# The RWKV-7 state chain laid out over both halves of the TensorE array

## The chip, the core and the metric

The kernel runs on one core of a Trainium2 chip. Its engines are TensorE (PE in the profile, with its weight loads as PEld), VectorE (DVE), ScalarE (ACT), GpSimd (POOL) and the queue that issues DMAs (SP). Each works through its own list of instructions in order and waits on semaphores for the others. The metric is the time of one execution in device microseconds (us).

## What is computed

One layer over 4096 tokens of 1024 features: a conditioned RMS norm, one input projection, a pooling branch, an RWKV-7 branch of 8 heads of 64, an output projection, the residual and a last norm. The change lies in the RWKV-7 branch:

```python
def step(S, inp):                        # per head; S is 64 x 64
    r_t, w_t, k_t, v_t, am_t, b_t = inp  # am = -kk, b = kk * a
    sa = jnp.einsum('bhij,bhj->bhi', S, am_t)
    S = (S * w_t[:, :, None, :]
         + sa[..., None] * b_t[:, :, None, :]
         + v_t[..., None] * k_t[:, :, None, :])
    y = jnp.einsum('bhij,bhj->bhi', S, r_t)
    return S, y
```

## The kernel before

Phase 1 makes the normed input and the pooling branch. Phase 2, the RWKV-7 branch, goes through 16 blocks of 256 tokens, each of 4 chunks of 64. Phase 3, the output projection, is spread into the last block and the tail.

A block has four parts. `front(b)` projects the block's input into 17 tiles of 128 features (`pj`, lines 570 to 572: eight steps of three f16 matmuls each); a step is a unit of fill. It is a generator: units of `front(b + 1)` are issued inside the other parts of block b by `fill(n)`, and so stand between their matmuls. Behind each group of four tiles (k, r, v, z of a head pair) come small products (`pl`, `pa`, `vps`, `pb`). `scores(b)` (lines 685 to 716) makes the 64x64 score matrices. `inverse(b)` (lines 728 to 784) inverts 32 triangular matrices: 30 steps on DVE (lines 746 and 751), two DVE transposes, then the products `qp` (line 774) and `m21p` (line 782). `chain(b)` (line 786 on) carries the state through the four chunks.

In a chunk the chain takes the heads in two groups of four. For each group it clears half a PSUM bank with a matmul of zeros (line 798), adds V to the scores (line 801, weights from rows 64 to 127), and multiplies the stored state by A and R of a pair in one matmul of 128x128 (line 806); `S` holds two heads of a pair on its diagonal, with zero blocks beside them. ACT copies the result out (`xa`, line 811), PE multiplies by the inverse (line 820), ACT copies that into `UV` (line 825) and scales S (line 831). Then PE makes the addition to S (line 835), which DVE adds (line 839), and the output y (line 846), which ACT copies (line 850). Four of every eight heads' products of lines 801 and 846 go to the same 64 output columns.

PE's order is that of a scheduler which takes instructions by the order written and by what is ready in its own plan; it may split a group. The counts of fill units are FS, FT, FA, FM, FB, FY, FC and the list FI. `ps_x` has two PSUM banks (`px`), `ps_pj` three.

Of the kernel before, what the change touches and what calls it, by code (L numbers as in the profile page):

```python
# [20 lines left out]
P = 128  # L21
# [3 lines left out]
NH = 8  # L25
# [11 lines left out]
# columns of the packed per-feature vectors  # L37
# [15 lines left out]
def kernel(  # L53
# [83 lines left out]
    with ExitStack() as ph:  # L137
# [10 lines left out]
        # -- c @ w_ada + b_ada, features on partitions --  # L148
# [21 lines left out]
        # evacuation scales: 1/(s_h s_w); z's goes into u's, and silu's half too  # L170
# [18 lines left out]
        def row_scale(b, ss):  # L189
            """[P, 4] sums of the rows' squares -> rows' 1/rms, broadcast over partitions"""  # L190
# [63 lines left out]
        def prep_u(q):  # L254
            """pooling weights: w_u @ blockdiag(pool_w), split into fp16 halves"""
# [48 lines left out]
        def gain():  # L304
            # |x| * rstd <= sqrt(D) bounds |h|
# [63 lines left out]
        def prep_gate():  # L369
            """gate, broadcast over partitions"""  # L370
# [11 lines left out]
        def prep_wo(k):  # L382
            """gate folded into w_out's columns, in two float32r parts"""
# [39 lines left out]
        def pooled(b, g, pu, tz):  # L423
# [5 lines left out]
            # trailing sums by doubling  # L429
# [14 lines left out]
        def side(b):  # L444
            """the later phases' weights, prepared along the way"""
# [46 lines left out]
    # =====================================================================  # L492
    # phase 2: RWKV-7 branch
    # =====================================================================
    with ExitStack() as ph:
# [10 lines left out]
        # block-of-ones, centering and per-head selectors  # L506
# [12 lines left out]
        # score mask [(b/k, s), (a/r, t)]: s < t for a, s <= t for r  # L519
# [26 lines left out]
        zw = k2c.tile([P, 64], F32, name="zw")  # L546
        G.memset(zw, 0.0)
# [7 lines left out]
        def front(b, f):  # L555
# [9 lines left out]
            def seg(m, name, bufs=1):  # L565
                pp = ps_pj.tile([P, TB2 + 1], F32, tag="pj", name=f"pj{b}_{m}")
                for k in range(KT):
                    if k:
                        yield
                    PE.matmul(pp, w2_hi[m][:, k, :], hh[k], start=(k == 0), stop=False)  # L570
# [26 lines left out]
            for p in range(NPAIR):  # L597
# [8 lines left out]
                # decay  # L606
# [65 lines left out]
        def scores(b, f, fill):  # L672
            AR, BK = f["AR"], f["BK"]
            # 1 / max(|kk|^2, eps^2): tokens on partitions, and instances on partitions
# [4 lines left out]
            for ch in range(NCH):  # L679
                # the two heads of a pair in turn: they use different rows of the array  # L680
# [16 lines left out]
                fill(2 * FS)  # L697
# [24 lines left out]
        def inverse(b, f, fill):  # L722
            """MT[:, i, :] = transpose of (I - D A)^-1 D, A strictly lower 64x64, D diagonal,
            per instance. Its two 32x32 diagonal blocks by elimination, an instance and a half of the
            rows per lane; the block below the diagonal by two products."""
# [3 lines left out]
            # both diagonal blocks of A^T side by side, then instances onto partitions  # L729
# [39 lines left out]
            fill(FT)  # L769
            pt = ps_sc.tile([P, 512], F32, tag="sc", name=f"qp{b}")  # L770
# [14 lines left out]

        def chain(b, f, fill):
            AR, UV, sc, BT, pc = f["AR"], f["UV"], f["sc"], f["BT"], f["pc"]
            MT = UV[0:64].rearrange("q c (h t) -> q (c h) t", h=NH)
            for ch in range(NCH):
                pxs, xas = [], []  # L790
                psn = ps_s.tile([P, NPAIR, HS], F32, tag="psn", name=f"psn{b}_{ch}")
                if ch % 2 == 0:
                    y = blk.tile([P, 512], F32, tag="y", name=f"y{b}_{ch}", bufs=3)
                for g in range(2):
                    # columns 0:256: A^T S and its additions (rows a, r); 256:512: U
                    px = ps_x.tile([P, 512], F32, tag="px", name=f"px{b}_{ch}_{g}")
                    pxs.append(px)
                    PE.matmul(px[64:128, 511:512], zw, zw[:, 0:1], start=True, stop=True, skip_group_check=True)  # L798
                    for j in range(4):
                        h = 4 * g + j  # L800
                        PE.matmul(  # L801
# [240 lines left out]
```

## Time and profile before

| | |
|---|---|
| time, median of 3 runs | 2221.42 us (2218.44 to 2222.96) |
| the profiled execution, its span from the first instruction to the last | 2223.1 us |
| PE busy | 2129.8 us (96%) |
| DVE busy | 1432.6 us (64%) |
| ACT busy | 1225.1 us (55%) |
| phase 2, from the first scores to the last output of the chain | about 455 to 1913 us |

The profile gives no other time of the profiled execution than its span. An x8 in a row of the timeline counts matmul records: an f32 matmul leaves two of them (two passes over its columns), an f16 matmul one. A row's second number runs to the end of the last result, and results overlap with the next matmul's start, so what a group occupies on PE is read from its start to the start of the next row.

### The profile page before, as it was taken

Reading aid. Unit: us, or ns where it says so; the run is one execution under the profiler, and the core shown is the slowest. Engines: PE = TensorE matmul, PEld = TensorE weight load, DVE = VectorE, ACT = ScalarE, POOL = GpSimd, SP = SyncE. Lnnn points to the kernel's source line nnn. Section 1 sums busy time; section 2 is a strip of 40 time slices with the busy share of each in tenths; the row PEclk is TensorE's granted clock in tenths of the full one; section 3 lists DMA queues with packets and bytes.
Section 4 is the critical chain, followed back from the end, with each engine's and each line's share of the span. In section 5 each row is a group of like instructions: output and inputs, shape, how many; then the busy total and the mean of one; then the engine's idle time right before and its main releaser. Section 6 shows DMA issues by size and latency. Waiting matters only on the chain. (4 is left out here: it accounts for less than half of the span.)

```text
span 2223.1 us, 46475 instructions
## 1 busy us (share of the span) xinstructions
PE 2129.8 (96%) x18906; PEld 1620.5 (73%) x18906; DVE 1432.6 (64%) x3407; ACT 1225.1 (55%) x2924; POOL 153.2 (7%) x271
## 2 busy tenths in 40 slices
PE   4999999999999999999999999999999999999998
PEld 2444444787787877878778777787787877788887
DVE  8898967575756757658477575675765847443433
ACT  3545433466676676666766667667676664422211
POOL 3000000000000000000000000000000000000000
PEclk7999999999999999999999999999999989999999
DMA  7867677000010000100100001000010423444432
GB/s 277 282 227 252 223 238 241 15 20 25 7 30 21 11 26 6 30 25 6 30 11 20 25 6 30 17 15 26 6 30 25 138 77 120 148 139 145 138 109 75
DMA packets 140440, 183.08 MB, mean 82 GB/s; under 512 B 12097, under 2 KB 94017, under 8 KB 140226
## 3 DMA queue, kind: packets, MB, share of 16 engines
q1 hardware_dynamic: 140226, 180.11, 24.8%
q8 instruction: 148, 2.42, 0.5%
q14 instruction: 66, 0.54, 0.1%
HBM read 121.22 MB, written 58.85 MB: 81 GB/s over the span
## 5 line engine op out<-in xcount | busy, mean ns | idle before, releaser
L570 PE MATMUL pj<-hh,w2h 128*128 128x257 f16 x2176 | 601.8, 277 | 1.0 <-ACT up L427 0.8
L572 PE MATMUL pj<-hh,w2l 128*128 128x257 f16 x2176 | 595.1, 273 | 0.0
L571 PE MATMUL pj<-hl,w2h 128*128 128x257 f16 x2176 | 593.4, 273 | 0.0
L570 PEld LDWEIGHTS <-w2h 128*128 128x128 f16 x2176 | 211.5, 97 | 53.8
L571 PEld LDWEIGHTS <-w2h 128*128 128x128 f16 x2176 | 214.6, 99 | 26.7 <-issue 1.3
L572 PEld LDWEIGHTS <-w2l 128*128 128x128 f16 x2176 | 210.2, 97 | 31.9
L942 PE MATMUL po<-wo,mh 128*128 128x512 f32 x512 | 204.4, 399 | 1.7 <-ACT mh L926 1.7
L943 PE MATMUL po<-wo,mh 128*128 128x512 f32 x512 | 202.1, 395 | 0.0
L413 PE MATMUL pp<-lo,w1h 128*128 128x512 f16 x512 | 194.7, 380 | 0.8 <-DVE lo L225 0.8
L414 PE MATMUL pp<-hi,w1l 128*128 128x512 f16 x512 | 194.4, 380 | 0.0
L412 PE MATMUL pp<-hi,w1h 128*128 128x512 f16 x512 | 194.0, 381 | 0.3 <-ACT hi L224 0.3
L948 ACT ACTIVATE sq<-x 128x512 f32<-128x512 f32 x64 | 40.4, 631 | 202.5 <-DVE x L946 200.3
L946 DVE TENSOR_TENSOR x<-po,x 128x512 f32<-128x512 f32 x64 | 44.2, 691 | 155.4 <-PE po L944 155.2
L839 DVE TENSOR_TENSOR S<-psn,S 64x256 f32<-64x256 f32 x128 | 53.9, 421 | 128.1 <-PE psn L835 127.3
L746 DVE TENSOR_TENSOR Wt<-W,Ab 128x30 f32<-128x30 f32 (+7 forms) x480 | 118.7, 247 | 17.9 <-ACT W L741 8.5
L751 DVE TENSOR_TENSOR W<-W,Wt 128x30 f32<-128x30 f32 (+7 forms) x480 | 117.9, 246 | 8.2
L714 ACT ACTIVATE bc<-BK,pc 128x128 f32<-128x128 f32 x256 | 91.8, 397 | 48.1 <-PE btp L715 27.3
L942 PEld LDWEIGHTS po<-wo,mh 128*128 128x128 f32 x512 | 96.9, 189 | 23.6 <-ACT mh L926 2.0
L943 PEld LDWEIGHTS po<-wo,mh 128*128 128x128 f32 x512 | 96.7, 189 | 22.4
L831 ACT ACTIVATE S<-S,pc 128x128 f32<-128x128 f32 x256 | 95.2, 397 | 28.9 <-PE px L806 28.4
L944 PE MATMUL po<-wo,ml 128*128 128x512 f32 x256 | 101.7, 399 | 0.0
L414 PEld LDWEIGHTS <-w1l 128*128 128x128 f16 x512 | 50.3, 98 | 61.3 <-issue 2.1
(278 smaller groups left out, 4318.9 us busy)
## 6 DMA issues: line engine op xcount, KB each, us to landing
x<-in_x_dram SPq DMA_DIRECT2D x64, 256.0 KB, 3.0
out_dram<-x SPq DMA_DIRECT2D x64, 256.0 KB, 2.1
xk<-in_xT_dram SPq DMA_DIRECT2D x56, 256.0 KB, 3.8
xt<-in_x_dram SPq DMA_DIRECT2D x28, 512.0 KB, 5.6
wada<-in_w_ada_dram SPq DMA_DIRECT2D x24, 512.0 KB, 6.8
w2raw<-in_w_in_dram SPq DMA_DIRECT2D x17, 512.0 KB, 5.5
hh<-hT_hi SPq DMA_DIRECT2D x32, 257.0 KB, 3.4
hl<-hT_lo SPq DMA_DIRECT2D x32, 257.0 KB, 3.0
```

Source lines behind the costliest of these rows:

```text
L412: PE.matmul(pp, w1_hi[m][:, k, :], hi, start=(k == 0), stop=False)
L413: PE.matmul(pp, w1_hi[m][:, k, :], lo, start=False, stop=False)
L414: PE.matmul(pp, w1_lo[m][:, k, :], hi, start=False, stop=(k == KT - 1))
L570: PE.matmul(pp, w2_hi[m][:, k, :], hh[k], start=(k == 0), stop=False)
L571: PE.matmul(pp, w2_hi[m][:, k, :], hl[k], start=False, stop=False)
L572: PE.matmul(pp, w2_lo[m][:, k, :], hh[k], start=False, stop=(k == KT - 1))
L746: V.tensor_mul(tmp[:, :n, :k], W[:, r0:, k : k + 1].to_broadcast([P, n, k]), Ab[:, k : k + 1, :k].to_broadcast([P, n, k]),)
L751: V.tensor_add(W[:, r0:, :k], W[:, r0:, :k], tmp[:, :n, :k])
L831: A.activation(S[:, p, :], S[:, p, :], AF.Identity, bias=0.0, scale=pc[:, p, ch : ch + 1])
L942: PE.matmul(po, mh[:, k, ts_], wo[0][k][n], start=(k == 0), stop=False)
L943: PE.matmul(po, mh[:, k, ts_], wo[1][k][n], start=False, stop=False)
L944: PE.matmul(po, (ml[:, k] if b % 2 == 0 else ml[k])[:, ts_], wo[0][k][n], start=False, stop=(k == KT - 1))
```

## The change

The state S loses its zero blocks: for each head pair it is 128 partitions by 64 columns, the even head on the lower 64 partitions and the odd head on the upper 64. The two `px` banks now stand for even and for odd heads and stay for a whole block; chunks take turns in their two halves of 256 columns. Every product of the chain is one of 64 columns that uses a quarter of the array (or, for lines 860 and 867, half of it), and neighbours in the order use different quarters. A chunk has three visits to the array's small tiles: A and R by S (line 833); the inverse's product together with the V products of the next chunk (lines 846 and 808); the additions to S and y (lines 860 and 867). The V products of chunk 0 are issued in `inverse`, ahead of `qp`. The clearing matmuls are gone. U is written to the upper half of the `psn` bank. The chain's matmuls, and the first fill matmul behind each visit, are kept in program order. The counts of fill units are others.

```diff
-    FS, FT, FA, FM, FB, FY, FC = 2, 5, 2, 1, 0, 1, 0
-    FI = [5 + ((i + 1) * 0 // 10 - i * 0 // 10) for i in range(17)]
+
+    FS, FT, FA, FB, FY = 2, 5, 2, 2, 2
+    FI = [5 - i % 2 for i in range(17)]
...
-        S = k2c.tile([P, NPAIR, P], F32, name="S")
+        S = k2c.tile([P, NPAIR, HS], F32, name="S")
...
-                fill(2 * FS)
+                fill(FS + 1)
...
+            f["px"] = [ps_x.tile([P, 512], F32, tag="px", name=f"px{b}_{hf}") for hf in range(2)]
+            run(lead(b, f, 0))
...
+        def ordered(mm):
+
+            pin[0] = True
+            return tc.keep_in_program_order(mm)
...
+            UV, sc, (pe, po) = f["UV"], f["sc"], f["px"]
+            par = 256 * (ch % 2)
+            for p in range(NPAIR):
+                for hf, px in ((0, pe), (1, po)):
+                    h, o = 2 * p + hf, 64 * hf
+                    ordered(PE.matmul(
+                        px[o : o + 64, par + p * HS : par + (p + 1) * HS], sc[64:128, ch * NH + h, 0:64],
+                        UV[64:128, ch, h * HS : (h + 1) * HS], start=(p == 0), stop=False, skip_group_check=True,
+                    ))
+                yield
...
-                    PE.matmul(px[64:128, 511:512], zw, zw[:, 0:1], start=True, stop=True, skip_group_check=True)
...
-                    for q in range(2):
-                        PE.matmul(
-                            px[:, q * P : (q + 1) * P], AR[:, 2 * g + q, ch].rearrange("q a t -> q (a t)"),
-                            S[:, 2 * g + q, :], start=False, stop=(q == 1), skip_group_check=True,
-                        )
...
+                    for ar in range(2):
+                        for hf, px in ((0, pe), (1, po)):
+                            o, ro = 64 * hf, 64 * (hf ^ ar)
+                            ordered(PE.matmul(
+                                px[ro : ro + 64, cs], AR[o : o + 64, p, ch, ar, :], S[o : o + 64, p, :],
+                                start=(p == 0 and ar == 1), stop=(ar == 0), skip_group_check=True,
+                            ))
...
+                    A.copy(xa, px[64 * hf : 64 * hf + 64, par : par + 256])
...
+                nl = lead(b, f, ch + 1) if ch + 1 < NCH else iter(())
+                for p in range(NPAIR):
                     for hf in range(2):
...
+                        ordered(PE.matmul(
+                            psn[64 * hf : 64 * hf + 64, uo + p * HS : uo + (p + 1) * HS],
+                            MT[:, ch * NH + 2 * p + hf, :], xas[hf][:, p * HS : (p + 1) * HS],
+                            start=True, stop=True, skip_group_check=True,
+                        ))
+                    run(nl, 1)
...
-                for hf in range(2):
-                    o = 64 * hf
-                    sv = S[o : o + 64, :, o : o + 64]
-                    V.tensor_add(sv, psn[o : o + 64], sv)
...
+                V.tensor_add(S, psn[:, 0:uo].rearrange("q (j e) -> q j e", e=HS), S)
+                for h in range(NH):
+                    hf, o = h % 2, 64 * (1 - h % 2)
+                    ordered(PE.matmul(
+                        (pe, po)[hf][o : o + 64, par + (h // 2) * HS : par + (h // 2 + 1) * HS],
+                        sc[:, ch * NH + h, 64:128], UV[:, ch, h * HS : (h + 1) * HS],
+                        start=False, stop=True, skip_group_check=True,
+                    ))
...
-                fill(FC)
+                fill(FY)
```

Where the instructions stand. On PE, before, in chunk 1 of block 2, at the start of the chunk (`px2_1_0` and `px2_1_1` are the two groups' banks, `pj3_16` a tile of the next block's projection):

```order
L798 MATMUL px2_1_0_7865<-zw_3686 64x1
L801 MATMUL px2_1_0_7865<-UV2_5631,sc2_6856 64x64 x4
L806 MATMUL px2_1_0_7865<-S_3690,AR2_5627 128x128 x2
L798 MATMUL px2_1_1_7875<-zw_3686 64x1
L801 MATMUL px2_1_1_7875<-UV2_5631,sc2_6856 64x64 x4
L806 MATMUL px2_1_1_7875<-S_3690,AR2_5627 128x128 x2
L570 LDWEIGHTS w2h16_2196
```

On PE, now, in the same chunk, the end of the first visit (`px2_0` is the even heads' bank, `px2_1` the odd heads'):

```order
L833 MATMUL px2_0_7664<-S_3688,AR2_5647 64x64
L833 MATMUL px2_1_7665<-S_3688,AR2_5647 64x64
L568 LDWEIGHTS w2h14_2188
L568 MATMUL pj3_14_7794<-hh3_1_6916,w2h14_2188 128x257
L569 LDWEIGHTS w2h14_2188
```

The second visit in the same chunk:

```order
L570 MATMUL pj3_14_7794<-hh3_1_6916,w2l14_2189 128x257
L846 MATMUL psn2_1_7854<-xa2_1_0_7871,UV2_5651 64x64
L846 MATMUL psn2_1_7854<-xa2_1_1_7873,UV2_5651 64x64
L808 MATMUL px2_0_7664<-UV2_5651,sc2_6898 64x64
L808 MATMUL px2_1_7665<-UV2_5651,sc2_6898 64x64
L846 MATMUL psn2_1_7854<-xa2_1_0_7871,UV2_5651 64x64
```

Line 833 has 16 matmuls in a row there, line 846 eight with eight of line 808 between them; the fill that stood behind the second group stands behind each visit.

On ACT, before, in chunk 1 of block 2, from the scaling of S to the copies into UV (`ta`, `rh` and `bc` belong to the next block's projection):

```order
L831 ACTIVATE S_3690<-S_3690,pc2_5630 128x128
L811 COPY xa2_1_0_7873<-px2_1_0_7865 64x256
L631 ACTIVATE ta3_3_7843<-ta3_3_7843,pv_3673 128x256
L831 ACTIVATE S_3690<-S_3690,pc2_5630 128x128
L811 COPY xa2_1_1_7883<-px2_1_1_7875 64x256
L831 ACTIVATE S_3690<-S_3690,pc2_5630 128x128 x2
L825 COPY UV2_5631<-px2_1_0_7865 64x2x64 x2
```

On ACT, now, from the copies of y of chunk 0 to the copies into UV of chunk 1:

```order
L874 COPY y2_0_7773<-px2_0_7664 64x4x64
L874 COPY y2_0_7773<-px2_1_7665 64x4x64
L617 ACTIVATE Pi3_3_7893<-L3_3_7890 128x256
L856 ACTIVATE S_3688<-S_3688,pc2_5650 128x64 x3
L840 COPY xa2_1_0_7871<-px2_0_7664 64x256
L840 COPY xa2_1_1_7873<-px2_1_7665 64x256
L856 ACTIVATE S_3688<-S_3688,pc2_5650 128x64
L572 ACTIVATE rS3_14_7881<-pj3_14_7794,c1_103 128x256
L853 COPY UV2_5651<-psn2_1_7854 64x4x64 x2
```

Three of the four scalings of S stand ahead of both copies `xa`, and one tile's evacuation ahead of the copies into UV.

On PE, before, the last rows ahead of `qp` of block 2 at the end of the inverse (21 matmuls of `pj3_14` stand between `pb3_2` and `qp2`; these are the last of them):

```order
L571 LDWEIGHTS w2h14_2188
L571 MATMUL pj3_14_7644<-hl3_1_6876,w2h14_2188 128x257
L572 LDWEIGHTS w2l14_2189
L572 MATMUL pj3_14_7644<-hh3_1_6874,w2l14_2189 128x257
L774 MATMUL qp2_7668<-MQ2_7651,sc2_6856 32x32 x32
```

On PE, now, the same place, from the last two of the eight V products of chunk 0:

```order
L808 MATMUL px2_0_7664<-UV2_5651,sc2_6898 64x64
L808 MATMUL px2_1_7665<-UV2_5651,sc2_6898 64x64
L661 MATMUL pb3_2_7731<-rh3_2_7608,bones_3649 128x256
L662 MATMUL pb3_2_7731<-rl3_2_7610,bones_3649 128x256
L774 MATMUL qp2_7674<-MQ2_7635,sc2_6898 32x32 x32
L568 LDWEIGHTS w2h13_2184
```

The projection stands 9 matmuls into tile 13 there instead of 21 into tile 14, and nothing stands between `pb3_2` and `qp2`. From the last scores of block 2 to its `qp` the order holds 276 `pj` matmuls now and 303 before; from there to the next block's last scores 132 now and 105 before.

## Rows read from the trace of the kernel before

**Rows 1.** The page: busy time and share of the span of each engine.

```profile
PE 2129.8 (96%) x18906; PEld 1620.5 (73%) x18906; DVE 1432.6 (64%) x3407; ACT 1225.1 (55%) x2924; POOL 153.2 (7%) x271
```

**Rows 2.** The four stretches of one block (from the inverse's first transpose on DVE to `qp`; from there to the chain; the chain; from the chain's end to the next block's first transpose). Columns: the stretch, its length, then busy time and count of PE, PEld, DVE, ACT and POOL, the granted clock of TensorE as a share of the full one, the DMA share and GB/s.

```profile
564.26:601.78 37.52, 35.38 (x301) 29.48 (x298) 35.76 (x109) 21.68 (x49) 2.05 (x8) 1.00 0.00 1
601.78:605.45 3.67, 3.67 (x146) 2.96 (x146) 1.00 (x3) 3.00 (x8) 0.75 (x1) 1.00 0.02 7
605.45:636.40 30.95, 30.01 (x368) 23.93 (x362) 11.07 (x24) 22.90 (x70) 2.07 (x2) 1.00 0.17 44
636.40:654.77 18.37, 18.37 (x178) 15.73 (x177) 12.03 (x26) 13.44 (x34) 1.64 (x1) 1.00 0.06 17
```

**Rows 3.** Timeline of PE through chunk 1 of that chain: start, length, line, operation, count.

```profile
613.38 0.23 PE L798 MATMUL px<-zw 128*64 128x1 f32 x2
...
616.59 0.27 PE L571 MATMUL pj<-hl,w2h 128*128 128x257 f16 x1
616.70 0.27 PE L572 MATMUL pj<-hh,w2l 128*128 128x257 f16 x1
616.91 0.45 PE L820 MATMUL px<-xa,UV 64*64 64x64 f32 x8
617.29 0.28 PE L570 MATMUL pj<-hh,w2h 128*128 128x257 f16 x1
...
620.70 0.28 PE L798 MATMUL px<-zw 128*64 128x1 f32 x2
```

**Rows 4.** Timeline of PE: the same operations in groups of other sizes, and the scores (line 685), whose two tiles go to two banks.

```profile
621.72 0.33 PE L801 MATMUL px<-UV,sc 64*64 64x64 f32 x2
621.97 0.71 PE L806 MATMUL px<-S,AR 128*128 128x128 f32 x4
622.61 0.56 PE L801 MATMUL px<-UV,sc 64*64 64x64 f32 x6
623.10 0.71 PE L806 MATMUL px<-S,AR 128*128 128x128 f32 x4
...
632.80 0.93 PE L685 MATMUL scp_sc<-AR,BK 64*128 64x128 f32 x6
633.66 0.68 PE L820 MATMUL px<-xa,UV 64*64 64x64 f32 x16
634.27 0.28 PE L570 MATMUL pj<-hh,w2h 128*128 128x257 f16 x1
...
640.03 0.37 PE L685 MATMUL scp_sc<-AR,BK 64*128 64x128 f32 x1
640.04 0.37 PE L685 MATMUL scp_px<-AR,BK 64*128 64x128 f32 x1
...
641.12 0.28 PE L570 MATMUL pj<-hh,w2h 128*128 128x257 f16 x1
```

**Rows 5.** Timeline of ACT at the start of that chain, and the PE row behind it with what ended its wait.

```profile
607.44 1.49 ACT L784 COPY UV<-m21p 32x256 f32<-32x256 f32 x4
608.96 0.63 ACT L811 COPY xa<-px 64x256 f32<-64x256 f32 x2
609.49 0.70 ACT L831 ACTIVATE S<-S,pc 128x128 f32<-128x128 f32 x2
...
609.47 0.45 PE L820 MATMUL px<-xa,UV 64*64 64x64 f32 x8 [0.94 <-ACT xa L811]
```

**Rows 6.** Groups by line: busy time, mean ns of one, idle time before them and its releasers, for the scaling of S and the addition to S.

```profile
L831 ACT ACTIVATE S<-S,pc 128x128 f32<-128x128 f32 x256 | 95.2, 397 | 28.9 <-PE px L806 28.4
L839 DVE TENSOR_TENSOR S<-psn,S 64x256 f32<-64x256 f32 x128 | 53.9, 421 | 128.1 <-PE psn L835 127.3
```

**Rows 7.** The end of the inverse: DVE's last instructions, and PE's.

```profile
597.35 0.48 DVE L575 SCALAR_TENSOR_TENSOR zS<-pj,c,zS 128x256 f32<-128x256 f32 x1
597.74 0.41 DVE L642 TENSOR_TENSOR rl<-rS,rh 128x256 fp32r<-128x256 f32 x1
600.49 1.23 DVE L768 STREAM_TRANSPOSE MQ<-UV 32x1024 f32<-32x1024 f32 x1
...
594.90 0.61 PE L650 MATMUL vps<-cmat,vS 128*128 128x128 f32 x4
...
598.34 0.28 PE L664 MATMUL pb<-rl,bones 128*128 128x256 f32 x1
...
601.78 0.75 PE L774 MATMUL qp<-MQ,sc 32*32 32x32 f32 x64 [0.82 <-DVE MQ L768]
```

**Rows 8.** Timeline of PE: a wait in phase 1.

```profile
343.19 1.11 PE L196 MATMUL pr<-ident,rs 128*128 128x128 f32 x4 [2.56 <-POOL rs L193]
```

**Rows 9.** Stretches (columns as in rows 2) around that wait and in the last block, between changes of the granted clock.

```profile
342.70:346.20 3.50, 3.01 (x10) 1.61 (x11) 3.47 (x7) 1.97 (x4) 0.43 (x1) 0.51 0.56 221
346.20:352.00 5.80, 5.80 (x28) 2.62 (x27) 5.24 (x10) 2.64 (x4) 0.00 (x0) 1.00 0.96 290
...
1817.30:1820.70 3.40, 2.53 (x21) 2.05 (x20) 2.55 (x7) 1.76 (x5) 0.77 (x1) 1.00 0.03 5
1820.70:1834.40 13.70, 12.01 (x56) 9.97 (x57) 5.88 (x8) 8.21 (x17) 0.00 (x0) 0.50 0.30 96
1834.40:1837.80 3.40, 3.40 (x9) 2.37 (x8) 2.36 (x3) 2.77 (x4) 0.00 (x0) 0.51 0.09 21
```

More of the change, by code (lines that the diff above doesn't have):

```diff
@@ L569, in seg @@
                         yield
-                    PE.matmul(pp, w2_hi[m][:, k, :], hh[k], start=(k == 0), stop=False)
+                    unpin(PE.matmul(pp, w2_hi[m][:, k, :], hh[k], start=(k == 0), stop=False))
                     PE.matmul(pp, w2_hi[m][:, k, :], hl[k], start=False, stop=False)
@@ L784, in inverse, with unpin, lead @@
                 A.copy(MT[0:32, 8 * q : 8 * q + 8, 32:64], pt[32 * q : 32 * q + 32, 0:256].rearrange("c (i t) -> c i t", t=32))
+        pin = [False]
+        def ordered(mm):
+            pin[0] = True
+            return tc.keep_in_program_order(mm)
+        def unpin(mm):
+            if pin[0]:
+                tc.keep_in_program_order(mm)
+                pin[0] = False
+        def lead(b, f, ch):
+            UV, sc, (pe, po) = f["UV"], f["sc"], f["px"]
[8 more added lines that the diff above has]
+                yield
         def chain(b, f, fill):
@@ L788, in chain @@
             MT = UV[0:64].rearrange("q c (h t) -> q (c h) t", h=NH)
+            pe, po = f["px"]
+            uo = 4 * HS
             for ch in range(NCH):
-                pxs, xas = [], []
-                psn = ps_s.tile([P, NPAIR, HS], F32, tag="psn", name=f"psn{b}_{ch}")
+                par = 256 * (ch % 2)
+                psn = ps_s.tile([P, 512], F32, tag="psn", name=f"psn{b}_{ch}")
                 if ch % 2 == 0:
                     y = blk.tile([P, 512], F32, tag="y", name=f"y{b}_{ch}", bufs=3)
-                for g in range(2):
-                    px = ps_x.tile([P, 512], F32, tag="px", name=f"px{b}_{ch}_{g}")
-                    pxs.append(px)
-                    PE.matmul(px[64:128, 511:512], zw, zw[:, 0:1], start=True, stop=True, skip_group_check=True)
-                    for j in range(4):
-                        h = 4 * g + j
-                        PE.matmul(
-                            px[0:64, j * HS : (j + 1) * HS], sc[64:128, ch * NH + h, 0:64],
-                            UV[64:128, ch, h * HS : (h + 1) * HS], start=(j == 0), stop=False, skip_group_check=True,
-                        )
-                    for q in range(2):
-                        PE.matmul(
-                            px[:, q * P : (q + 1) * P], AR[:, 2 * g + q, ch].rearrange("q a t -> q (a t)"),
-                            S[:, 2 * g + q, :], start=False, stop=(q == 1), skip_group_check=True,
-                        )
-                    xa = blk.tile([64, 256], F32, tag=("W", "Wt")[g], name=f"xa{b}_{ch}_{g}")
-                    A.copy(xa, px[0:64, 0:256])
@@ L812, in chain @@
+                xas = []
+                for hf, px in ((0, pe), (1, po)):
+                    xa = blk.tile([64, 256], F32, tag=("W", "Wt")[hf], name=f"xa{b}_{ch}_{hf}")
+                    A.copy(xa, px[64 * hf : 64 * hf + 64, par : par + 256])
                     xas.append(xa)
                 fill(FA)
-                for g in range(2):
-                    px, xa = pxs[g], xas[g]
-                    if g:
-                        fill(FM)
-                    for j in range(4):
-                        o, c = 64 * (j % 2), 256 + HS * (j // 2)
-                        PE.matmul(
-                            px[o : o + 64, c : c + HS], MT[:, ch * NH + 4 * g + j, :],
-                            xa[:, j * HS : (j + 1) * HS], start=(j % 2 == 0), stop=True, skip_group_check=True,
-                        )
-                    for hf in range(2):
-                        A.copy(
-                            UV[0:64, ch, 256 * g : 256 * g + 256].rearrange("q (j f e) -> q j f e", f=2, e=HS)[:, :, hf],
-                            px[64 * hf : 64 * hf + 64, 256:384].rearrange("q (j e) -> q j e", e=HS),
-                        )
+                nl = lead(b, f, ch + 1) if ch + 1 < NCH else iter(())
@@ new lines, in chain @@
+                for p in range(NPAIR):
+                    for hf in range(2):
+                        ordered(PE.matmul(
[4 more added lines that the diff above has]
+                    run(nl, 1)
+                for hf in range(2):
+                    A.copy(uv[:, :, hf], psn[64 * hf : 64 * hf + 64, uo:].rearrange("q (j e) -> q j e", e=HS))
@@ L941, in project @@
                     for k in range(KT):
-                        PE.matmul(po, mh[:, k, ts_], wo[0][k][n], start=(k == 0), stop=False)
+                        unpin(PE.matmul(po, mh[:, k, ts_], wo[0][k][n], start=(k == 0), stop=False))
                         PE.matmul(po, mh[:, k, ts_], wo[1][k][n], start=False, stop=False)
```

24 lines of the change are left out of this document (10 added, 14 removed).

## The prediction

> **What bounds the kernel now.** I read the page first: PE is busy 96% of the span [rows 1], so a cut in PE's work can shorten the kernel, where no other engine takes over at once. The stretches of one block come next [rows 2]. They add up to 90.5 us and are not alike. In the inverse (37.52 us) DVE is busy 35.76 us and PE 35.38 us: both are full, and DVE has no spare time. In the other three (3.67 + 30.95 + 18.37 = 52.99 us) PE is busy all the time but for one wait of 0.94 us, for ACT's copy xa [rows 5], and DVE is busy for only 24.1 us of the 53. So 53 us of a block end with PE, and 37.5 us with DVE. The timeline of a chunk then shows what PE does there, and the rows of ACT how near the next bound lies: ACT is busy for 22.90 us of the chain's 30.95 us.
>
> **What the chain costs on PE now.** Chunk 1 takes 613.38 to 620.70, 7.32 us [rows 3]. In it stand 12 fill matmuls, at a step of 0.111 us (616.59 to 616.70) 1.33 us, which leaves 5.99 us for the chain. Chunk 0 has about 1.0 us less (its first zeros and three V products already ran in the inverse), and chunk 3 about 0.8 us less (lines 820 of both groups in one visit of 16 [rows 4]). Four chunks: 4 x 5.99 - 1.8 = 22.2 us.
>
> **What it costs after.** Rows 4 give the price of a pass over 64 columns. Six passes of line 801, all in the same quarter of the array, take 0.49 us (622.61 to 623.10) and two take 0.25 us: 0.06 us each. Line 820 alternates two column halves: 16 passes take 0.61 us (633.66 to 634.27), 8 take 0.38 us [rows 3], so 8 more cost 0.23 us, two per 0.058 us, and a group has 0.15 us besides. Coming from the fill costs another 0.10 us: line 820 starts 0.21 us behind the last fill matmul instead of 0.11 [rows 3]. The scores alternate row halves that write two banks, and their tiles start 0.01 us apart (640.03 and 640.04): row halves run beside each other as well. No row shows all four quarters at once. The bounds are four per 0.058 us and two per 0.058 us; I take four, because both directions are in the rows and the new order puts the four quarters next to each other with the row halves in different banks.
>
> A visit with line 833 or lines 846 and 808 (32 passes): 0.10 + 0.15 + 8 x 0.058 = 0.72 us, or 1.18 us by the other bound. Lines 860 and 867 use all 128 rows, two halves at a time: 32 passes, 0.25 + 16 x 0.058 = 1.18 us. A chunk has 2.62 us, four have 10.5 us, and a projection product that stands between two of line 846 in chunk 0 adds two changes of tile, 0.2 us: 10.7 us. The saving is 11.5 us of PE's work a block. The V products of chunk 0 move into the inverse for the zeros and V products that stood there; that is a draw.
>
> The scores of chunk 0 stood in pieces between the chain's groups, 16 passes one at a time, 0.14 us each (six in 0.86 us, 632.80 to 633.66); now they alternate, 1.09 us (640.03 to 641.12 [rows 4]): 1.2 us less.
>
> **Fill that moves.** 27 projection matmuls a block go from the inverse to the other stretches (105 become 132 between qp and the next scores): 3.0 us. There PE is the bound and pays them. In the inverse PE gets 3.0 us shorter, and nothing comes of it: DVE's 30 steps, its transposes and the evacuations remain. Only what stands behind one more tile in DVE's order goes: zS and szt now follow the last transpose, and one evacuation comes in ahead, 0.35 us less of 37.5 [rows 7]. I take 37.2 us.
>
> **New waits in the chain.** Before, two groups of heads covered each other's copies. Now all heads wait together, and only six fill matmuls (0.67 us) lie behind each visit. Chunk 1, from the first matmul of line 833, by the durations of rows 5: pair 0 is done at about 0.4 us. ACT has three scalings of S ahead of xa in its order. The new scaling is half as wide; bounds 0.20 us, half of rows 6, and the whole 0.40 us; I take 0.36 us with a step of 0.27, as two copies xa have (0.63 us for two). So S runs to 1.36, the xa copies to 1.90, and PE starts 0.14 us later (xa ends at 609.32, line 820 starts at 609.47), at 2.04. Without the wait it would be ready at 0.62 + 0.67 + 0.10 = 1.39: wait 0.65 us. Visit to 2.66; the U copies 2.85 to 3.5; line 860 at 3.6 instead of 3.43: 0.2. Visit to 4.7; then line 833 of the next chunk waits for both copies of y, since they read the banks it writes: 5.65 instead of 5.47, 0.2. DVE's addition, one of 0.42 us [rows 6], is done before that. So chunk 1 waits 1.05 us. Chunk 2 is alike, the square of y in front of its first scaling: 1.2 us. Chunk 0 waits for m21p's four copies (1.49 us) before xa, and y stands behind a projection's exponential: 1.4 us in all. Chunk 3 has the four normalised outputs ahead of xa: 0.5 us. Together 4.1 us a block, where one wait of 0.94 was.
>
> **The sum.** PE's work outside the inverse: 52.05 - 11.5 - 1.2 + 3.0 = 42.35 us; with waits 46.45 instead of 52.99: 6.5 us less. With the inverse's 0.35: 6.9 us a block, 15 blocks 103 us. In block 15 the fill is the output projection, whose 512-column matmuls are longer and cover the waits: its chain gives its 11.5 us and a little, 12 us. Together 115 us.
>
> One cost stands against it. After the DVE transposes PE has little left: vps needs vS, then 9 matmuls (1.0 us) and the V products (0.7), while pb waits for rl. Before, vps ran at 594.90, 6.8 us ahead of the transpose's end [rows 7]; now, from there, PE is done about 4 us before the end, and rl comes only one transpose (1.2 us) before it: some 2.9 us of waiting in one piece, then 0.8 us more. In phase 1 a wait of 2.56 us [rows 8] was followed by 3.5 us at a granted clock of 0.51, the lower of the two levels (1.2 instead of 2.4 GHz), and dense matmuls brought it back [rows 9]. At the lower clock the 15 fill matmuls behind qp take 1.7 us more, of which the four copies of MQ cover a part. I take 1 us in half of the blocks: 8 us.
>
> 2223.1 - 115 + 8 = 2116 us by the profiled span. The median of the runs is 1.7 us below that span: **2114 us**. The saving in PE's work alone would be 12.7 us x 16 = 203 us; half of it is lost on the DVE-bound inverse and the copies. The likeliest case's own range is 2085 to 2145 us, with the waits between 2 and 6 us a block.
>
> **Rivals.**
>
> Quarters run only two at a time. Lines 833 and 846/808 cost 1.18 instead of 0.72 us, 0.92 us a chunk. Of that the scalings of S, which run beside line 833, hide about a quarter: 0.7 x 64 = 45 us, 2159 us. For it: no row with four. Against it: rows 4 in both directions. The Trainium skill, "TensorEngine Tiling (Array Packing)", Restrictions and Gotchas, says that two row tiles cannot use one PSUM bank at a time; the order keeps them in different banks, and by that rule four would run.
>
> The inverse isn't bound by DVE, and the waits shrink: were PE's cut to come through whole, 2020 us. For it: the two engines are nearly equal there. Against it: DVE's 35.76 us busy. Half way from the forecast lies 2065 us.
>
> Slower: the clock falls in the wait at the inverse's end and stays at the lower level through the chain. In the last block it fell after 2.53 busy us of 3.40 and stayed at 0.50 for 17 us, over small matmuls with waits, until dense ones came (1820.7 to 1837.8 [rows 9]). The chain now is just such work. At half clock its 21 us of PE work and the 3 us of qp and m21p take 24 us more, less the 4 us of waits that this covers: 20 - 7 = 13 us a block more than before, 2223 + 16 x 13 = 2430 us if it is every block. It is slower than before once more than about 15 us of each block run at the lower clock. Against it: six fill matmuls follow each visit, and the chain of before, with a 0.94 us wait, kept 1.00 [rows 2]. The Trainium skill, "TensorE: Matmul & The Clock Gate", HAM oscillation, warns that a loop with waits between short bursts of matmuls drops back each time; by that this rival would be the forecast, and the granted 1.00 over the chain of rows 2 speaks against it.
>
> That the change doesn't do what it says: the order shows the three visits unbroken but for the one product in chunk 0; little is left for this.
>
> **Chances.** The forecast's case 0.62; quarters by twos, or waits of like size, 0.15; more of PE's cut coming through 0.13; the clock low for a part of the chain, still faster, 0.03; low through the chain, slower, 0.06; no change 0.01. A difference of 0.2% is about what a measurement of this kernel can tell. Faster 0.93, same 0.01, slower 0.06. The range takes in half of the second rival and the first: 2055 to 2170 us.
>
> **What would show it.** Right: a block of about 83 to 84 us; line 833 in about 0.6 us for 32 records; line 846 waiting for xa and line 833 for y; PE idle some 4 to 5 us in an inverse that still takes 37 us with DVE full; ACT the busiest engine in the chain. Wrong: line 833 at 1.1 us (quarters by twos), an inverse several us shorter, or a granted clock near 0.5 in the stretch behind qp.

## The result, and the profile after

Measured: 2159.8 us (median of 4 runs, 2154.0 to 2163.0) against 2222.2 us before on the same chip (2218.4 to 2225.4). The ratio is 0.9717, its 95% interval 0.9699 to 0.9734. The profiled spans are 2158.6 and 2223.1 us. The change brought 62 us where 108 were forecast; the time lies inside the range of 2055 to 2170 us.

The page of the changed kernel, against [rows 1]: PE is busy for 93% of the span instead of 96%, so part of the work that PE was spared came back as waiting. The row PEclk (the granted clock in 40 slices of the span) has eights where the kernel before had nines; the mean granted clock fell from 0.989 to 0.963. The first PEclk row is that of the kernel before.

```profile
span 2158.6 us, 48872 instructions
PE 2002.1 (93%) x20186; PEld 1497.8 (69%) x20186; DVE 1393.9 (65%) x3343; ACT 1190.7 (55%) x2796; POOL 150.9 (7%) x270
PEclk7999999999999999999999999999999989999999
PEclk7999999998989999999999899998999989999999
```

The four stretches of one block after, with the columns of [rows 2]: inverse, qp to chain, chain, scores.

```profile
647.81:685.35 37.54, 33.47 (x289) 27.77 (x286) 35.25 (x108) 22.11 (x49) 2.27 (x8) 1.00 0.01 2
685.35:690.09 4.74, 4.74 (x144) 3.40 (x144) 1.17 (x4) 2.34 (x6) 0.42 (x1) 0.64 0.01 3
690.09:714.10 24.01, 21.77 (x453) 17.08 (x446) 9.48 (x21) 19.54 (x58) 2.07 (x2) 1.00 0.11 32
714.10:733.50 19.40, 18.20 (x189) 15.16 (x186) 11.57 (x25) 14.87 (x37) 1.64 (x1) 1.00 0.18 45
```

The chain fell from 30.95 to 24.01 us, the largest gain. The inverse kept its length, although PE has 2 us less to do there. Two stretches got longer: from qp to the chain 3.67 became 4.74 us, at a mean clock of 0.64, and the scores went from 18.37 to 19.40.

The next rows are the waits of PE between 500 and 1720 us, fourteen blocks: who waited for whom, us in total, times, longest.

```profile
PE pb L661 <- ACT rh L638: 35.4, 28, 1.4
PE scp_sc L683 <- DVE sc L690: 16.8, 14, 1.2
PE psn L846 <- ACT xa L840: 15.6, 37, 1.0
PE pb L662 <- DVE rl L640: 10.0, 14, 0.7
PE qp L774 <- DVE MQ L766: 9.8, 13, 0.8
```

Before, the only repeated wait outside the inverse was the one for xa, 0.94 us [rows 5]. Half of the 28 waits for rh stand in the middle of the inverse, the other half at its end. The first row is one in the middle; the clock stayed at 1.00 there. The others are the end, where PE's timeline has three waits in a row; they answer to [rows 7], where the only wait was 0.82 us:

```profile
657.61 0.39 PE L661 MATMUL pb<-rh,bones 128*128 128x256 f32 x1 [1.39 <-ACT rh L638]
...
681.31 0.68 PE L808 MATMUL px<-UV,sc 64*64 64x64 f32 x16
683.11 0.38 PE L661 MATMUL pb<-rh,bones 128*128 128x256 f32 x1 [1.12 <-ACT rh L638]
684.21 0.38 PE L662 MATMUL pb<-rl,bones 128*128 128x256 f32 x1 [0.71 <-DVE rl L640]
685.35 0.75 PE L774 MATMUL qp<-MQ,sc 32*32 32x32 f32 x64 [0.76 <-DVE MQ L766]
```

Behind that place the clock is low in every block. Two blocks next to each other, each as the stretch from qp to the chain and the chain with its way to the first score pass:

```profile
856.74:862.11 5.37, 5.35 (x144) 3.97 (x144) 1.48 (x4) 2.34 (x6) 0.44 (x1) 0.50 0.00 0
862.11:889.12 27.01, 26.23 (x468) 19.98 (x461) 9.35 (x21) 20.88 (x61) 1.82 (x2) 0.85 0.12 32
944.72:949.48 4.76, 4.74 (x143) 3.41 (x143) 1.20 (x4) 2.35 (x6) 0.44 (x1) 0.64 0.01 3
949.48:974.83 25.35, 23.12 (x468) 17.75 (x460) 9.63 (x21) 20.69 (x61) 2.07 (x2) 1.00 0.13 34
```

The first block was at the lower of the two levels for 13.65 us and takes 88.0 us from qp to qp, the second for 3.41 us and takes 85.7 us. The 2.3 us between them are in these two stretches (0.61 and 1.66 us). Before, no low stretch stood between 500 and 1720 us; after, 99 us of them. (The 87.6 and 85.6 to 86.0 us in the first expectations below are block lengths from one m21p to the next, though they say qp.)

The last new wait, 1.20 us, is in the scores. PE's row and DVE's rows of one block:

```profile
720.26 0.37 PE L683 MATMUL scp_sc<-AR,BK 64*128 64x128 f32 x1 [1.20 <-DVE sc L690]
...
718.58 0.69 DVE L891 TENSOR_TENSOR y<-y,rstd 128x512 f32<-128x512 f32 x1 [1.75 <-POOL rstd L889]
719.19 0.42 DVE L645 SCALAR_TENSOR_TENSOR szt<-tz,zS 128x256 f32<-128x256 f32 x1
719.52 0.68 DVE L690 TENSOR_TENSOR sc<-scp_sc,mask 128x512 f32<-128x512 f32 x1
```

The scores of chunk 0 were in their bank at 716.6. DVE stood still for 1.75 us, waiting for POOL's rstd (the factor that normalises y) with line 891 at the head of its order; the mask products (line 690) were queued behind it, and the scores of chunk 1 need the same banks. Before, the same multiplication (line 867 there) waited too, but stood behind the mask products of chunk 0:

```profile
638.71 0.69 DVE L692 TENSOR_TENSOR sc<-scp_px,mask 128x512 f32<-128x512 f32 x1
...
641.23 0.69 DVE L867 TENSOR_TENSOR y<-y,rstd 128x512 f32<-128x512 f32 x1 [1.42 <-POOL rstd L865]
```

### The profile page after: what moved, and what is told of

The parts are those of the page before. It is cut to its first block, busy times and chain, and to the rows that moved or that the text cites. A ratio compares the mean times of both kernels' runs of the same rounds, so it can differ in the third digit from the quotient of the medians.

```text
span 2158.6 us, 48872 instructions
## 1 busy us (share of the span) xinstructions
PE 2002.1 (93%) x20186; PEld 1497.8 (69%) x20186; DVE 1393.9 (65%) x3343; ACT 1190.7 (55%) x2796; POOL 150.9 (7%) x270
## 5 line engine op out<-in xcount | busy, mean ns | idle before, releaser
L568 PE MATMUL pj<-hh,w2h 128*128 128x257 f16 x2176 | 615.8, 283 | 0.8 <-ACT up L427 0.8
L570 PE MATMUL pj<-hh,w2l 128*128 128x257 f16 x2176 | 608.9, 280 | 0.0
L569 PE MATMUL pj<-hl,w2h 128*128 128x257 f16 x2176 | 607.5, 279 | 0.0
L568 PEld LDWEIGHTS <-w2h 128*128 128x128 f16 x2176 | 215.6, 99 | 59.5
L570 PEld LDWEIGHTS <-w2l 128*128 128x128 f16 x2176 | 215.5, 99 | 36.1
L569 PEld LDWEIGHTS <-w2h 128*128 128x128 f16 x2176 | 218.9, 101 | 27.1 <-issue 1.1
L613 DVE TENSOR_TENSOR_SCAN L<-rst,tw 128x256 f32<-128x256 f32 x64 | 43.7, 683 | 82.4 <-ACT tw L611 82.4
L683 PE MATMUL scp_sc<-AR,BK 64*128 64x128 f32 x512 | 75.6, 289 | 18.7 <-DVE sc L690 18.7
```

Source lines behind the costliest of these rows:

```text
L568: unpin(PE.matmul(pp, w2_hi[m][:, k, :], hh[k], start=(k == 0), stop=False))
L569: PE.matmul(pp, w2_hi[m][:, k, :], hl[k], start=False, stop=False)
L570: PE.matmul(pp, w2_lo[m][:, k, :], hh[k], start=False, stop=(k == KT - 1))
```

## The experiments

Three causes were to be told apart: the fall of the clock, the order on DVE at the scores, and the order on ACT in the chain. Times are medians; the kernel before, timed beside them, took 2221.6 to 2223.8 us.

### Fill put back

```diff
-    FS, FT, FA, FB, FY = 2, 5, 2, 2, 2
-    FI = [5 - i % 2 for i in range(17)]
+    FS, FT, FA, FB, FY = 2, 5, 2, 1, 1
+    FI = [5 for i in range(17)]
```

> The changed kernel with the fill counts of before alone put back: 100 steps of fill in the inverse instead of 92, 16 in the chain instead of 24. The changed kernel takes 86.3 us from one qp to the next on average: 87.6 where the clock was low for 13.65 us there, 85.6 to 86.0 where it was low for 3.41 us. Theory A (the fall of the clock at the inverse's end is what the prediction mis-sized, about 2.2 us a block over a floor near 84): eight steps of 0.33 us fill the 2.6 us in which PE waits at the inverse's end, the clock stays at 1.00 there, and the low stretches near the qp passes vanish; the chain loses 2.7 us of fill a block and pays it back in waits on ACT. 84 to 85 us a block, 2125 to 2145 us in all. Rival B (the clock costs little, the waits inside the chain decide): the chain's new waits cost all that the inverse gains or more, 86 to 88 us a block, 2155 to 2185 us.

Measured 2139.4 us, ratio 0.9630 (0.9617 to 0.9643); 85.6 us a block. From the V products to the chain it is 4.17 us instead of 8.7 to 9.4, at full clock; but the clock fell later instead, in the first chunk of the chain, behind a wait of 1.32 us for xa:

```profile
861.70 0.57 PE L846 MATMUL psn<-xa,UV 64*64 64x64 f32 x3 [1.32 <-ACT xa L840]
...
862.40:865.90 3.50, 2.96 (x54) 2.29 (x45) 1.97 (x5) 2.11 (x7) 0.00 (x0) 0.51 0.02 5
```

PE's waits are 94 us in all, smaller rows counted, as in the changed kernel; the longest are others:

```profile
PE psn L846 <- ACT xa L840: 22.0, 27, 1.3
PE pb L661 <- ACT rh L638: 20.7, 15, 1.4
PE ytp L903 <- DVE y L891: 19.1, 14, 1.4
PE psn L860 <- ACT UV L853: 16.3, 29, 1.0
```

With eight steps less fill (2.7 us) the chain is not shorter: 25.5 us to the first score pass at the least, 25.4 in the changed kernel where the clock stayed up. The steps that the change put there lie in waits. The edit also let the wait of the scores go (ytp, which transposes y, waits for the same y instead), so it settles nothing about the clock.

### PE kept busy, with 18 multiplications and with 15

```diff
+            for i in range(18):
+                ordered(PE.matmul(
+                    f["px"][0][:, 256 + 128 * (i % 2) : 384 + 128 * (i % 2)], cmat, ident,
+                    start=True, stop=True, skip_group_check=True,
+                ))
             run(lead(b, f, 0))
```

> The changed kernel with 18 multiplications of constants (128x128 f32, some 0.15 us each, 2.7 us in all) put on TensorE behind the last fill before the qp passes, into columns of a bank that are written over later; nothing reads them. They do no work and only keep PE busy in the wait for MQ. Theory A (clock): the granted clock stays at 1.00 through qp, the inverse keeps its 37.5 us, and what stands behind runs at full clock: 84 to 84.5 us from qp to qp instead of 86.3, 2120 to 2135 us. Rival B (the low clock lies beside work that ACT and DVE bound and costs nothing): 2155 to 2165 us. Rival C (the passes run later than the wait is long): slower by up to 1 us a block, 2175 us.

Measured 2143.0 us, ratio 0.9651 (0.9637 to 0.9664). The clock stays at 1.00: 6.8 us of low stretches between 500 and 1720 us instead of 99, and nearly all blocks take 85.0 us. The time lies above theory A's range: the 18 took 4.1 us, not 2.7 (a product of 128 f32 columns has two records of 0.114 us, and the expectation took a record of line 648 for a product), and ran past the wait. So they were cut to 15, with no other edit:

> The changed kernel with 15 multiplications of constants in the wait for MQ and no other edit: the price of the clock by itself, without the 0.55 us a block by which 18 of them ran past the wait. Theory A (the clock's price and the wait of the scores make up the 46 us by which the prediction was too low): 7 us under the run with 18, as in the kernel with the two order edits (2114.1 to 2106.9), so 2136 us; the price of the clock is then 24 us, and what is left over the forecast of 2114 us is the scores' wait, 15 x 1.27 us and what it costs in the last block. Rival B (the overrun was hidden here, behind the scores' wait): 2143 us, and 5 to 10 us of the miss stay without a cause.

Measured 2135.0 us, ratio 0.9606 (0.9592 to 0.9621); 84.5 us in thirteen of the first fourteen blocks. That is theory A, which said 2136. PE's timeline of one block (the 15 are 30 records):

```profile
840.52 3.51 PE L770 MATMUL px<-ident,cmat 128*128 128x128 f32 x30
...
844.73 0.75 PE L779 MATMUL qp<-MQ,sc 32*32 32x32 f32 x64
847.42 0.75 PE L787 MATMUL m21p<-UV,MQ 32*32 32x32 f32 x64
848.11 0.69 PE L838 MATMUL px<-S,AR 64*64 64x64 f32 x32
```

From qp to the chain it is 3.38 us now, where the changed kernel has 4.6 to 5.6. Work that nobody needs saves 25 us: that is the price of the clock. The two pb products, which stood between the V products and qp, are behind qp now; qp waited for MQ in any case, so this is not where the gain comes from.

### The scaling of the state on DVE

```diff
-                for p in range(NPAIR):
-                    A.activation(S[:, p, :], S[:, p, :], AF.Identity, bias=0.0, scale=pc[:, p, ch : ch + 1])
...
-                V.tensor_add(S, psn[:, 0:uo].rearrange("q (j e) -> q j e", e=HS), S)
+                for p in range(NPAIR):
+                    V.scalar_tensor_tensor(S[:, p, :], S[:, p, :], pc[:, p, ch : ch + 1], psn[:, p * HS : (p + 1) * HS], op0=ALU.mult, op1=ALU.add)
```

> The changed kernel with the scaling of the state taken off ACT (four activations a chunk, 1.17 us) and folded into DVE's addition (four multiply-adds of 128x64 instead of one add of 128x256, 0.40 us). Theory A (ACT's order in a chunk makes the chain's waits: in chunks 1 and 2 three of these four stand between the y copies and the xa copies): xa starts 0.7 us earlier there and the chain is 0.8 to 1.5 us a block shorter, 2137 to 2150 us. Rival B (the state's addition takes 0.3 us more a chunk, and the next chunk's passes wait for it): no gain, 2155 to 2180 us. The clock stays as it is in either.

Measured 2134.8 us, ratio 0.9607 (0.9594 to 0.9620). It looks like theory A and is not: the stretch from the first score pass to the V products before qp fell from 51.54 to 50.28 us, and the chain by only 0.2 us where the clock was up. PE's waits for xa did fall, from 15.6 us in fourteen blocks to 5.1:

```profile
PE psn L846 <- ACT xa L840: 5.1, 5, 1.2
```

The scheduler, given other work, had also put DVE's order at the scores right:

```profile
708.88 0.68 DVE L690 TENSOR_TENSOR sc<-scp_sc,mask 128x512 f32<-128x512 f32 x1
709.63 0.43 DVE L645 SCALAR_TENSOR_TENSOR szt<-tz,zS 128x256 f32<-128x256 f32 x1
709.98 0.68 DVE L690 TENSOR_TENSOR sc<-scp_px,mask 128x512 f32<-128x512 f32 x1
710.91 0.68 DVE L890 TENSOR_TENSOR y<-y,rstd 128x512 f32<-128x512 f32 x1
```

### The mask products first

```diff
+                if ch == 0:
+                    first[0] = last_sc.ins
...
-            V.tensor_mul(
+            with tc.issue_after(first[0]):
+                V.tensor_mul(
```

> The changed kernel with one place of DVE's order put back: the multiplication of y by its rstd, which stands ahead of the mask products of the next block's chunk 0 and waits 1.75 us for POOL, goes behind them again. Theory A (this order makes the wait of 1.20 us at the score passes of chunk 1 in each block): that wait goes, the scores take 18.2 us instead of 19.4, and the time falls by 15 x 1.2 = 18 us to about 2142 us. Rival B (PE gets the same wait one step later, at btp or at the next mask products): 2155 to 2165 us.

Measured 2135.0 us, ratio 0.9609 (0.9592 to 0.9627). The wait is gone from PE's list, and the stretch up to the V products is 50.28 us here too. The gain is 25 us, more than the 18 of theory A, of which some 4 are in the last block, although the clock is low for longer (133 us between 500 and 1720).

### Both together, and with the other edits

> The scaling of the state on DVE and the mask products first, nothing else: the other two runs of this call less their third edit. If the two edits are separate 2110 us (83.7 us a block); if both are worth the same wait of ACT and DVE 2130 us. Whatever it gives, the step from here to the run with the 18 multiplications is the price of the clock alone in a kernel with shorter waits: 17 us if as in the changed kernel, 0 if the clock no longer falls.

Measured 2134.9 us, ratio 0.9599 (0.9585 to 0.9613): as either alone. With line 891 out of the way in both, moving the scaling off ACT is worth nothing that can be measured at this clock. ACT's order does make most of the chain's waits for xa (5.1 us here too, 10.4 with the mask products alone); what has fallen is that the chain's length hangs on them.

> The scaling of the state on DVE, the mask products first, and the 18 multiplications of constants in the wait for MQ; the fill counts are those of the changed kernel. Theory A (clock and order are separate costs): 17 + 25 + 25 us off, 2093 us, 82 us a block, no low stretch between 600 and 1700 us. Rival B (the gains of the two order edits came from the places where the clock was low, so that they overlap with the clock's): 2110 to 2125 us.

Measured 2114.1 us, ratio 0.9507 (0.9492 to 0.9523); 83.56 us in most blocks. The number lies in rival B's range, but not for its reason: the multiplications take off 20.8 us here and 16.8 alone, the order 28.9 us here and 25 alone. Theory A's 2093 counted the order's 25 us twice, once for each of two edits that do the same. The clock and the scores are separate causes.

> As the run with the scaling on DVE, the mask products first and 18 multiplications of constants (2114.1 us), with 15 of them. In its trace the 18 took 4.1 us (0.228 us each, not 0.15), MQ was there at 843.36 and qp started at 843.91: the multiplications and the eight V products behind them ran 0.55 us past the wait. Theory A (what overran was on the path, and 0.5 us of idle PE does not bring the clock down): qp 0.5 us earlier in each block, 83.05 us a block, about 2106 us. Rival B (a short wait is left before qp and the clock falls again): low stretches come back, 84 us a block or more, 2115 to 2135 us.

Measured 2106.9 us (2104.6 to 2108.6), ratio 0.9478 (0.9465 to 0.9491). That is theory A, and beats both kernels, the changed one by 53 us. Its four stretches have 1.00 throughout:

```profile
717.93:755.55 37.62, 36.06 (x318) 30.82 (x315) 35.33 (x108) 22.14 (x49) 2.27 (x8) 1.00 0.01 2
755.55:758.91 3.36, 3.36 (x145) 2.96 (x146) 1.31 (x4) 2.35 (x6) 0.42 (x1) 1.00 0.02 5
758.91:782.86 23.95, 22.36 (x458) 17.26 (x450) 10.41 (x31) 16.04 (x42) 2.07 (x2) 1.00 0.10 23
782.86:800.97 18.11, 18.11 (x185) 15.15 (x182) 11.99 (x28) 14.88 (x37) 1.64 (x1) 1.00 0.22 58
```

Beside the changed kernel, the second is 1.38 us shorter (the clock) and the fourth 1.29 us (the order on DVE). Inverse and chain are as they were, the chain with ACT at 16.04 us instead of 19.54: ACT's load alone is not what sets its length.

> Three edits together: the scaling of the state on DVE, the mask products of chunk 0 ahead of the multiplication by rstd, and the fill counts of before (100 steps in the inverse, 16 in the chain). Theory A (three causes that add up): 20 + 25 + 25 us off the 2159.8 us of the changed kernel, about 2090 us, 82 us a block, at a clock that still falls for one stretch of 3.41 or 6.83 us in most blocks. Rival B (PE's work is the floor: 78 us of it stand in a block of 86, and waits that are taken away in one place come back in another, as the fill is the same): 2110 to 2130 us.

Measured 2137.3 us, ratio 0.9611 (0.9597 to 0.9626): outside both ranges, and only 2 us better than the fill put back alone. Real fill taken from the chain for the wait before qp opens waits in the chain, and the clock is low there (64 us between 500 and 1720). Beside the 2134.9 us of the same two edits, moving the fill as the change did is worth 2 us in the new layout.

### The quarters one behind the other

```diff
-                for p in range(NPAIR):
...
-                    for ar in range(2):
-                        for hf, px in ((0, pe), (1, po)):
+                for hf, px in ((0, pe), (1, po)):
+                    for ar in (1, 0):
+                        for p in range(NPAIR):
```

> The changed kernel with the 32 passes of line 833 in another order: all eight of one quarter of the array one behind the other, then those of the next quarter, instead of one on each quarter in turn. The same passes on the same data. Theory A (the quarters run at once, and the change's gain rests on that): the group takes 32 x 0.058 us = 1.85 us instead of 0.69, by the step of six passes of one quarter in the kernel before; 4 x 16 groups cost 1.15 us more each, some 70 us, 2215 to 2240 us. Rival B (the passes are short of something else, such as their issue, and the order is no matter): 2155 to 2170 us.

Measured 2175.0 us, ratio 0.9781 (0.9760 to 0.9801): neither. The groups of line 833 by operation, first of the changed kernel, then of this one (the first number is busy time in us):

```profile
L833 PE MATMUL px<-S,AR 64*64 64x64 f32 x2048 | 54.9, 234 | 0.5
```

```profile
L833 PE MATMUL px<-S,AR 64*64 64x64 f32 x2048 | 107.0, 236 | 0.0
```

The same 2048 records take twice as long one behind the other: the quarters do run at once. A group takes 1.54 us at full clock, not the 1.85 expected:

```profile
1037.47 1.54 PE L833 MATMUL px<-S,AR 64*64 64x64 f32 x32
```

Yet of 52 us of PE work only 15 came out as time. The same with the clock kept up:

> The passes of line 833 one quarter of the array behind the other, as in the run where that alone was done (2175.0 us), together with the 18 multiplications of constants of the run that kept the clock up (2143.0 us). The order of the quarters adds 52 us of busy PE over the kernel (54.9 to 107.0 us for this line). Theory A (behind the change the chain is bound by its round trips through ACT, and PE has time to spare in it): 0.2 us a block over 2143, 2143 to 2150 us; the 15 us that it cost before were the clock's. Rival B (PE's passes are still on the path): 0.8 us a chunk, 3.3 us a block, 2185 to 2200 us.

Measured 2144.1 us, ratio 0.9647 (0.9634 to 0.9660), against 2143.0 without the edit; 85.27 us a block instead of 85.02. The line takes 98.4 us here instead of 53.6, and next to nothing of that is on the path. The product behind the wait for xa (line 851 in both), first without the edit, then with it:

```profile
L851 PE MATMUL psn<-xa,UV 64*64 64x64 f32 x1024 | 62.5, 227 | 27.8 <-ACT xa L845 23.6
L851 PE MATMUL psn<-xa,UV 64*64 64x64 f32 x1024 | 49.0, 224 | 4.2 <-ACT xa L845 4.2
```

The wait for xa fell from 23.6 to 4.2 us, and the time of the product itself, with the pauses between its records, from 62.5 to 49.0: the longer passes lie where PE had waited.

### The fill alone, in the kernel before

```diff
-    FS, FT, FA, FM, FB, FY, FC = 2, 5, 2, 1, 0, 1, 0
-    FI = [5 + ((i + 1) * 0 // 10 - i * 0 // 10) for i in range(17)]
+    FS, FT, FA, FM, FB, FY, FC = 2, 5, 2, 1, 1, 2, 0
+    FI = [5 - i % 2 for i in range(17)]
...
-                fill(2 * FS)
+                fill(FS + 1)
```

> The kernel before with the change's fill counts alone: 92 steps in the inverse instead of 100, 24 in the chain (two more a chunk), 5 a chunk in the scores; layout, passes and order of the state chain as before. Theory A (before, the chain is PE's own work end to end, so what is added to it is paid in full, and the inverse, which DVE bounds, gives nothing back but opens a wait at its end): chain 2.7 us a block longer, inverse still 37.5, and the clock falls at its end as it does in the changed kernel: 93 to 95 us from qp to qp instead of 90.5, 2255 to 2295 us. Rival B (the fill only changes places): 2215 to 2230 us.

Measured 2310.4 us, ratio 1.0387 (1.0369 to 1.0404), 96.2 us a block: slower even than theory A. From qp to the chain's end, scores and inverse of one block, then the part of it at the lower clock, and qp itself:

```profile
700.95:741.44 40.49, 40.49 (x529) 31.71 (x529) 13.13 (x29) 25.48 (x76) 2.24 (x3) 0.87 0.09 23
741.44:758.54 17.10, 16.92 (x172) 14.39 (x172) 11.01 (x24) 13.53 (x34) 1.64 (x1) 1.00 0.14 41
758.54:796.13 37.59, 33.65 (x286) 28.21 (x283) 35.30 (x108) 22.14 (x49) 2.27 (x8) 1.00 0.01 2
...
702.20:712.50 10.30, 10.30 (x117) 7.77 (x117) 0.90 (x2) 5.70 (x17) 0.00 (x0) 0.50 0.01 2
```

```profile
796.13 0.75 PE L774 MATMUL qp<-MQ,sc 32*32 32x32 f32 x64 [2.46 <-DVE MQ L768]
```

PE is busy all of the 40.49 us (34.62 us before, [rows 2]): no wait is left there in which the fill and the low clock could lie. The wait before qp and the low clock behind it come with the fill counts, not with the layout.

## Why the prediction was right, and where it failed

**The stretches outside the inverse.** Forecast 46.45 us, measured 48.15 in the block shown (4.74 + 24.01 + 19.40), and 45.42 in the last kernel (3.36 + 23.95 + 18.11), without the low clock and the wait of the scores. The sum came out nearer than its parts, which is in part luck: PE was busy for 44.71 us of the 48.15 (forecast 42.35; 1.4 us of the difference is the low clock), and it stood idle for 2.24 us of the chain (forecast 4.1). Four quarters do run at once: 32 records of line 833 take 0.69 us where nothing holds them up (forecast 0.72). On average they take 0.86 us (54.9 us in 64 groups), pauses between them counted, so part of the forecast waits stands inside the visits. But the passes of line 833 were not the bound: with the clock kept up, nearly doubling their time cost 0.25 us a block. What sets the chain's length instead is not shown. Its round trips through the other engines are the likely answer, but the one edit that took work off ACT left the chain at 23.95 us, and the passes of the other visits were not made longer in any run. So the rival "quarters only two at a time" had the wrong price. Its 2159 us is what was measured, by accident; its mechanism was not there, and line 833, even at one quarter at a time, costs those 0.25 us a block, and 15 us in all where the clock is not kept up.

**The inverse.** Forecast 37.2 us and bound by DVE, measured 37.54 (37.59 and 37.62 in the other kernels shown): right in kind. The 0.35 us from the shifted evacuation did not come.

**The fill.** "There PE is the bound and pays them" was wrong for the chain: eight of its 24 steps taken away made it no shorter. It is right of the kernel before, where the same fill made things worse.

**The clock: the term that was mis-sized.** The prediction saw the wait at the inverse's end, put it at 2.9 us in one piece and 0.8 more, and took "1 us in half of the blocks: 8 us". The wait is 2.6 us in three pieces, the clock falls behind it in every block, and keeping PE busy there gives back 25 us (2159.8 to 2135.0): 1.2 us in a block with 3.41 us of low clock, 3.5 us in one with 13.65. So the wait was put too long and its price too low. The slower rival, a clock low through the whole chain, did not come: in phase 2 it was at most 13.65 us in a row. The Trainium skill, "TensorE: Matmul & The Clock Gate", HAM oscillation, tells of loops whose waits between short bursts bring the clock down each time; the trace agrees for the end of the inverse and, with the fill put back, for the first chunk, while the chain from 690.09 to 714.10, with its waits for xa, kept 1.00.

**The scores: the term that was missing.** The sum took the stretch's PE work and no wait; DVE "busy for only 24.1 us of the 53" was taken as free. Its order there was read for what had to be done, not for what would wait at its head. Line 891 ahead of the mask products costs 1.27 us a block.

Together, kernels without the low clock and without that wait take 2106.9 us; the forecast was 2114. The 46 us that were missed are these two: 25 us for the clock, and 28 us for the order on DVE with the scaling (2135.0 to 2106.9), less the 7 us by which the rest was forecast too high. In that second step the first fourteen blocks give 83.2 instead of 84.6 us; some 5 us come in the last block, for which no cause is shown. What the scaling has of the 28 us at full clock was not measured by itself; the way from the chain's start to the first score pass, where it stands, got 0.2 us a block shorter.

Not settled: what sets the chain's length, why the clock stays low for 13.65 us in some blocks and 3.41 in others, and why the scheduler put line 891 first in the changed kernel and not in the one with the scaling on DVE.

## What to carry to other kernels

Where PE's fill is moved out of a stretch that another engine bounds, look at what PE does at its end: a wait that is itself hidden can still cost a low clock behind it, and work without use can pay there. A stretch in which an engine is nearly always busy may yet hide waits in which more work would fit; double the work and see whether the time follows before counting on a cut. And when an edit helps, look at whether the scheduler moved something else with it: here two edits gave the same 25 us by the same accident of order.

## What was not expected of the hardware

In every block, three waits of 1.12, 0.71 and 0.76 us with 0.4 us products between them were followed by a granted clock of 0.50. The length of one wait does not tell: in the same kernel the single waits of 1.39 us in the middle of the inverse and of 1.20 us at the scores left the clock at 1.00, as those of 0.82 and 0.94 us did in the kernel before, while with the fill put back one of 1.32 us was followed by 0.51. Eight passes of 64 x 64 in a row on each quarter of the array take 1.54 us for 32, less than 32 steps of 0.058 us: the first of a group start 0.058 us apart, as in the kernel before, but later ones partly in pairs, 0.004 to 0.006 us apart.
